# Bias tables ahead of x in SyncE's queue, three late W_up chunks, one product ahead of the first row factors, and remainders moved in W_out's second half

## The chip, the core and the metric

The kernel runs on one core of one Trainium2 chip. The metric is the time of one execution in device microseconds; lower is better. TensorE (PE) multiplies, VectorE (DVE) and ScalarE (ACT) do elementwise work, GpSimd (POOL) does small vectors and some transfers, and SyncE (SP) issues most DMAs.

## The reference

One encoder layer on a sequence of 512 positions and 1024 channels, in float32:

```python
h = rms_norm(x, attn_norm_g)
xr, gate, q, k, v = split(h @ w_in)             # 512 columns each
xr = centred_depthwise_conv(xr, conv_w, conv_b)
y_rnn = (rg_lru(xr, fwd) + rg_lru(xr, bwd)) * gelu(gate)
y_attn = dilated_attention(q, k, v, rel_bias)   # 8 heads, three dilated windows
mix = concat(rms_norm(y_rnn), rms_norm(y_attn))
x = x + mix @ w_out
x = x + square(relu(rms_norm(x) @ w_up)) @ w_down
return rms_norm(x)
```

## The kernel before, in words

**Products in three parts.** Every float32 operand is split into a rounded part and a remainder, `hi` and `lo`; `mm3` (L322 to L325) makes one product of three matmuls: hi·hi, hi·lo, lo·hi. A weight chunk of 128 x 1024 goes through three steps: a load into `wraw`, `tw` or a piece of `ws`; `conv_hi` (L252, on ACT, a few on DVE) writes `whi`; `conv_lo` (L279, on DVE) writes `wlo` as the difference. `whi` and `wlo` have four buffers each and `wraw` has three, so a step waits until the step or product that used the buffer before has gone by. `remake` (L262, L264) is another way to a remainder: ACT writes the negative rounded part, and a POOL transfer adds the raw chunk to it.

**Who sets the order.** On PE, ACT, DVE and POOL the order of the program is the order of the engine. SP's queue is ordered by the framework and runs ahead of the other engines; its issues wait only for buffers and for the landing of DMAs issued earlier. `emit_dma` (L230) issues the next chunk of the list `plain` into a `wraw`; it is called by `conv_lo`, so that each chunk that is done fetches another. The list runs over w_in, w_v, w_out and then w_up.

**Start.** x arrives transposed, in eight pieces, with the first columns of w_in. `cvx` splits them, and PE multiplies (`pxr`, four banks of PSUM). The sums of squares are turned by PE (`pcs`, L441), added by DVE (`cs`, `rv`), raised to the power -0.5 by POOL (`rcol`, L428, 128 x 4), turned back by four transposes (`prow`, L420) and copied by ACT (`rrow`): the first row factors. `xmm` makes the products of the fourth bank, k = 1 to 7, around that place. Convolution (`conv_a`, `conv_b`, L516 to L525) and the gates' products (`pg`, L544) follow.

**Attention.** For a pair of heads and a block of queries, `att_s` (L830) makes the scores in two banks, one for each head, and `att_e` (L847) adds the bias and takes the minimum on DVE and the exponential on ACT. The bias comes as a table for each head and parity in a `tw` buffer; `load_tw` fetches it with two DMAs from `nbd` in DRAM (L496, 192 KB, and L498, 160 KB). There are four `tw` buffers. Between these steps `fill` draws from a list of products (`pqk`, and `pwo` of W_out's first half) and `add_x` draws from the list `more`. `load_x` fills `more` with the loads of x in rows (`x_in`, L1078, 256 KB each), of blocks of W_out (`w_in`, L1081, 512 KB each), and sums of these (`sum1` to `sum3`).

**W_out's second half** takes seven steps, `OSEQ = 11, s2, s3, s4, 21, s1, 22`, of four products each. `wo_x` (L1231) adds a finished bank to x. The steps 11, s2, s3 and s4 use the same pair of banks, so a product of s2 waits until `wo_x` has read what 11 left there; and `wo_x` needs the factors of the attention half, `rc[1]`, which come over the same way as the first: `pcs`, `cs`, `rv`, POOL's `rcol`. `BES` names what is done beside each product: `conv_hi`, `conv_lo`, the remainders `o_lo`, `o_lo2` (L931, L937) of the attention output, and `st["wo"]`, which adds the last bank of W_out's first half to x (L1014). Then come w_up and w_down, which the diff does not touch.

Of the kernel before, what the change touches and what calls it, by code (L numbers as in the profile page):

```python
# [12 lines left out]
FT = mybir.dt.float32  # L13
# [4 lines left out]
P = 128  # L18
# [85 lines left out]
def hybrid_kernel(ctx: ExitStack, tc, xw0, xw, xn, w_in, w_v, w_out, w_up, w_dn, gates, vecs, rel, onehot, fg, out):  # L104
# [13 lines left out]
    def g_(name, dt=FT, shape=(P, S)):  # L118
        return work.tile(list(shape), dt, name=name, tag="g", bufs=NG)
# [111 lines left out]
    def emit_dma():  # L231
        if plain:
            i = plain.popleft()
            r = stream.tile([P, 1024], FT, name="wraw", tag="wraw", bufs=3)
            nc.sync.dma_start(r, source(chunks[i]))
            raws[i] = r
# [8 lines left out]
    def conv_hi(i):  # L245
        if i < len(chunks):
            i = swap.get(i, i)
            hi = stream.tile([P, 1024], FR, name="whi", tag="whi", bufs=4)
            if i in ON_DVE:
                nc.vector.tensor_copy(hi, raws[i])  # L250
            else:
                act(hi, raws[i], AF.Copy)  # L252
            splits[i] = (hi,)
# [9 lines left out]
        for n, t in enumerate(remade[i]):  # L263
            nc.gpsimd.dma_start(f(t), raws[i][:, n * S:(n + 1) * S], accum_op=OP.add)  # L264

    def emit_plain(i):
        if chunks[i] == ("o", "11"):
            emit_dma()

    def conv_lo(i):  # L270
        if i < len(chunks):
            i = swap.get(i, i)
            r = raws.pop(i)
            if i in remade:
                splits[i] += (remade.pop(i),)
                emit_plain(i)
                return
            lo = stream.tile([P, 1024], FR, name="wlo", tag="wlo", bufs=4)
            nc.vector.tensor_tensor(lo, r, f(splits[i][0]), op=OP.subtract)  # L279
            splits[i] += (lo,)  # L280
            c = chunks[i]
            if isinstance(c, tuple) and c[0] == "o":
                if c[1] == "11":
                    emit_dma()
            elif isinstance(c, tuple) and len(c) == 4:
                h, kind, f0 = c[:3]
                if kind == "t1" and cq[h, f0, "t2"] not in raws:
                    nc.gpsimd.dma_start(r, ublock(h, "22", f0), accum_op=OP.add)
                    raws[cq[h, f0, "t2"]] = r
                elif kind == "22":  # L290
                    t = raws[cq[h, f0, "t3"]]
                    nc.vector.tensor_tensor(t, t, r, op=OP.add)
                elif kind in ("t2", "21"):
                    held[kind] = r
                    if len(held) == 2:
                        t = held.pop("t2")
                        nc.vector.tensor_tensor(t, t, held.pop("21"), op=OP.add)
                        raws[cq[h, f0, "t4"]] = t
                        emit_dma()
                if kind in ("11", "22"):  # L300
                    emit_dma()
            elif isinstance(c, tuple) and c[1][0] == "s":
                nxt = {"s1": ("s2", "22"), "s2": ("s4", "21")}.get(c[1])
                if nxt:
                    nc.gpsimd.dma_start(r, wblock(c[0], nxt[1], c[2]), accum_op=OP.add)
                    raws[cd_[c[0]] + {"s2": 2 * NQ + 2 * c[2], "s4": 6 * NQ + c[2]}[nxt[0]]] = r
            else:
                emit_dma()

    def feed(c, k):  # L310
# [24 lines left out]
    h_lo = big.tile([P, KD, S], FR, name="h_lo", tag="bigB")  # L335

    XW, XG = S + 3 * P, S + KD
    xwt, w3 = [], []
    for k in range(KD):
        if 4 <= k < 7:  # L340
            xwt.append(stream.tile([P, 1024], FT, name="wraw", tag="wraw", bufs=3)[:, :XW])
        else:
            xwt.append(work.tile([P, 1024], FT, name="tw", tag="tw", bufs=4)[:, :XW if k else XG + 3 * P])
        if k == 0:
            nc.sync.dma_start(xwt[0][:, :XG], xw0[:, :XG])
            nc.sync.dma_start(xwt[0][:, XG:], xw0[:, XG:])
            w03 = g_("w03")[:, :P]
            nc.sync.dma_start(w03, w_in[3][:, :P])
        else:
            nc.sync.dma_start(xwt[k], xw[k - 1])  # L350
        if k == 6:
            nc.sync.dma_start(vt, vecs)
    ag = consts.tile([P, KD], FT, name="ag")
    nc.gpsimd.tensor_copy(ag, xwt[0][:, S:XG])

    sqx = {}

# [318 lines left out]
    def xmm(ks):  # L676
        for k in ks:
            mm3(pxr[3], wk(3, k), hk(k), False, k == KD - 1)
# [7 lines left out]
    for i in range(2):  # L686
        nc.gpsimd.dma_start(oht[i], onehot[:, i * S:(i + 1) * S])
    conv_lo(4)
    xmm(range(1, 2))
    rstd = row_tile(rcol, "et")  # L690
    conv_a(0, pxr[0])
    conv_a(1, pxr[1])
# [1 line left out]
    cneg, chalf = next(spc)  # L694
    conv_b(0)
    act(warm, epsb, AF.Sigmoid)
    xmm(range(2, KD))
    conv_a(2, pxr[2])
    conv_a(3, pxr[3])
    conv_lo(5)  # L700
# [232 lines left out]
    def o_hi2(k):  # L933
        act(o_tiles(k)[0], at[2 + k], AF.Copy)
# [74 lines left out]
    def wo_thunks():  # L1009
        order = [(0, tt, k) for tt in range(4) for k in range(4)] + [(1, tt, k) for h in (0, 2) for tt in range(4) for k in (h, h + 1)]  # L1010
        pw = {}

        def end(n, tt):
            stt(x1[tt, n], pw[n, tt], rc[0][:, tt:tt + 1], x1[tt, n], op0=OP.mult, op1=OP.add)  # L1014

        def mk(b, n, tt, k):
            def run():
                if k == 0:
                    pw[n, tt] = ps_("pwo", "pj")
                o = pw[n, tt]  # L1020
                hi, lo = splits[C_WO + 2 * n + k // 2]
                sl, tsl = slice((k % 2) * S, (k % 2 + 1) * S), slice(tt * P, (tt + 1) * P)
                mm3(o, [t[:, tsl] for t in ycat[k]], (hi[:, sl], lo[:, sl]), k == 0, k == 3)
                if b in (1, 15, 18, 28):
                    conv_hi(C_WO + {1: 3, 15: 4, 18: 5, 28: 6}[b])
                if b in (3, 17, 20):
                    conv_lo(C_WO + {3: 3, 17: 4, 20: 5}[b])
                if n == 0 and tt and k == 3:
                    end(0, tt - 1)
                if n and (tt, k) == (0, 1):  # L1030
                    end(0, 3)
                if n and k == 3 and tt < 3:
                    end(1, tt)
            return run
        st["wo"] = lambda: end(1, 3)
        return [mk(b, *o) for b, o in enumerate(order)]
# [11 lines left out]
    def fill(n):  # L1048
        for _ in range(n):
            if fillers and fillers[0] is None:  # L1050
                fillers.popleft()
                load_x()
            if fillers:
                fillers.popleft()()
# [12 lines left out]
    def load_x():  # L1067
        xb = big.tile([P, KD, S], FT, name="x1", tag="bigA")
        ws = big.tile([P, 4, 1024], FT, name="ws", tag="bigB")
        b12, b22, b21, s1 = [ws[:, i, :] for i in range(4)]  # L1070
        tt = nc.vector.tensor_tensor

        def chunk(n, t):
            raws[C_WA + OSEQ.index(n)] = t

        def x_in(g, n):
            x1[g, n] = xb[:, 2 * g + n, :]
            return lambda: nc.sync.dma_start(x1[g, n], xn[2 * g + n])  # L1078

        def w_in(t, b):  # L1080
            return lambda: nc.sync.dma_start(t, oblock(b))  # L1081

        def sum1():
            tt(s1, b12, raws[C_WA], op=OP.add)

        def sum2():
            t = work.tile([P, 1024], FT, name="tw", tag="tw", bufs=4)
            tt(t, s1, b22, op=OP.add)
            chunk("s2", t)
            t4 = work.tile([P, 1024], FT, name="tw", tag="tw", bufs=4)  # L1090
            chunk("s4", t4)
            more[1].append(lambda: tt(t4, t, b21, op=OP.add))

        def sum3():
            tt(b12, b12, b22, op=OP.add)

        for n, t in (("s3", b12), ("22", b22), ("21", b21), ("s1", s1)):
            chunk(n, t)
        w_in(b12, "12")()
        x_in(0, 0)()  # L1100
        more.append([x_in(1, 0), w_in(b22, "22")])
        more.append([x_in(2, 0), x_in(3, 0)])
        more.append([sum1, w_in(b21, "21")])
        more.append([sum2, x_in(0, 1)])
        more.append([sum3, x_in(1, 1)])
        more.append([x_in(2, 1), x_in(3, 1)])

    def rnn_end(t):
        last[t]()
# [137 lines left out]
        nc.vector.tensor_tensor(hb["l"][k], hm[k], f(hb["h"])[:, k, :], op=OP.subtract)  # L1247

    fill(1)
    att_av(3, range(4))  # L1250
    fill(1)
    o_sum("s1", 1)
# [5 lines left out]
    fill(3)  # L1258
    rc[1] = rstd_cols(row_sums(turned(ssy[1], "gs")), S)
    fill(1)  # L1260
    conv_lo(C_WA + 2)
    remake(C_WA + OSEQ.index("21"))
    fill(len(fillers))
    nrc = consts.tile([P, 4], FT, name="nrc")
# [3 lines left out]
        return {0: lambda: conv_hi(C_WA + j), 3: lambda: conv_lo(C_WA + j)}  # L1268

    BES = {w: cv(i + 3) for i, w in enumerate(OSEQ)}  # L1270
    BES["11"].update({1: lambda: (o_hi2(1), remake(C_WA + OSEQ.index("s1"))), 3: lambda: st["wo"]()})
    BES["s2"].update({1: lambda: conv_lo(C_WA + 3), 2: lambda: o_hi("s1", 1), 3: lambda: (conv_lo(C_WA + 4), o_lo2(0))})
    BES["s3"].update({1: lambda: o_lo2(1)})
    BES["s4"].update({1: lambda: (o_lo("s1", 0), o_sum("22", 1)), 2: lambda: o_hi("22", 1)})
    BES["21"].update({1: lambda: o_lo("s1", 1), 3: lambda: (conv_lo(C_WA + 7), o_lo("22", 0), o_lo("22", 1))})
    BES["s1"].update({1: lambda: h2_t(0, "pj"), 2: lambda: h2_t(1, "pj"), 3: lambda: (conv_lo(C_WA + 8), h2_l(0))})
# [558 lines left out]
```

## Time and profile before

| | us |
|---|---|
| median of 3 runs | 535.21 |
| lowest and highest | 534.62, 536.07 |
| profiled execution, its own time | 536.4 |
| span of its profile, first to last instruction | 534.6 |
| PE busy | 525.5 |
| DVE busy | 434.6 |
| ACT busy | 359.1 |
| POOL busy | 72.3 |

The profile is of one execution. The mean granted clock of TensorE is 0.999 of full speed. A line of the timeline gives the start, the duration, the engine, the line of the kernel, the operation, what it writes and reads, and in brackets how long the engine was idle before and what ended that. SPq marks the issue of a DMA, not its transfer. The end of a matmul is modelled, so what a wait cost PE is read from the starts of two matmuls that follow each other.

### The profile page before, as it was taken

What the parts mean: (1) busy time and instruction counts of PE and PEld (TensorE: products, weight loads), DVE (VectorE), ACT (ScalarE), POOL (GpSimd) and SP (SyncE); (2) the same over time, 40 slices, a digit from 0 to 9 for tenths busy, and PEclk for the clock granted to TensorE, in tenths of its full rate; (3) what the DMA queues carried; (4) which work ended last, traced back from release to release, by engine and by line L of the source; (5) the groups of instructions that cost most, each with busy time, mean ns of one, the idle gap of its engine ahead of it and who ended that gap; (6) DMA issues with size and microseconds to landing.
All of it is one profiled execution on the core that took longest, in us unless ns stands there. A gap on an engine that the chain in (4) does not pass through costs nothing.

```text
span 534.6 us, 8387 instructions
## 1 busy us (share of the span) xinstructions
PE 525.5 (98%) x3035; PEld 451.3 (84%) x3035; DVE 434.6 (81%) x640; ACT 359.1 (67%) x578; POOL 72.3 (14%) x121
## 2 busy tenths in 40 slices
PE   9999999999998999999999999999999999999995
PEld 7756888887886778889999888888999999888884
DVE  5999788986866789889769986879756987987885
ACT  6578946787865666587567755566657686755664
POOL 0282000000100051001030213001101110131000
PEclk9999999999999999999999999999999999999999
DMA  8754386598687259956595899995978496799704
GB/s 280 220 151 139 81 228 186 158 242 216 148 287 245 67 90 207 366 199 167 153 191 165 201 262 275 292 347 114 289 229 209 115 217 193 176 297 258 192 1 158
DMA packets 42602, 107.05 MB, mean 200 GB/s; under 512 B 4916, under 2 KB 15284, under 8 KB 42560
## 3 DMA queue, kind: packets, MB, share of 16 engines
q1 hardware_dynamic: 34848, 80.14, 46.0%
q0 software_dynamic: 7536, 26.14, 26.3%
q8 instruction: 24, 0.39, 0.3%
q10 hardware_dynamic: 176, 0.23, 0.1%
q14 instruction: 18, 0.15, 0.1%
HBM read 94.92 MB, written 4.23 MB: 185 GB/s over the span
## 4 chain that ended last, share of the span: by engine, by line
PE 85%; issue 8%; DVE 3%; DMA 1%; POOL 1%; SPq 0%; ACT 0%; DVEq 0%; POOLq 0%; ACTq 0%
PE pu L324 10%; PE pu L323 10%; PE pu L325 10%; PE pd L323 9%; PE pd L324 9%; PE pd L325 9%; PE pqk L323 3%; PE pqk L325 3%; PE pqk L324 3%; PE ps L830 2%; PE pv L323 2%; PE pg L544 1%; PE pv L324 1%; PE pp L323 1%; PE pp L325 1%
## 5 line engine op out<-in xcount | busy, mean ns | idle before, releaser
L279 DVE TENSOR_TENSOR wlo<-wraw,whi 128x1024 fp32r<-128x1024 f32 x71 | 86.7, 1221 | 23.2 <-ACT whi L252 22.8
L252 ACT ACTIVATE whi<-wraw 128x1024 fp32r<-128x1024 f32 x67 | 70.8, 1059 | 37.0 <-PE pd L325 19.3
L324 PE MATMUL pd<-wlo,ah 128*128 128x512 f32 (+1 forms) x195 | 75.3, 386 | 0.0
L323 PE MATMUL pd<-whi,ah 128*128 128x512 f32 (+1 forms) x195 | 75.3, 386 | 0.0
L325 PE MATMUL pd<-whi,al 128*128 128x512 f32 (+1 forms) x195 | 75.3, 386 | 0.0
L252 ACT ACTIVATE whi<-tw 128x1024 fp32r<-128x1024 f32 x38 | 40.2, 1060 | 39.4 <-DMA tw<-in_w_up_dram 12.0
L324 PE MATMUL pu<-hl,whi 128*128 128x256 f32 x224 | 63.5, 283 | 0.0
L325 PE MATMUL pu<-hh,wlo 128*128 128x256 f32 x224 | 63.4, 283 | 0.0
L323 PE MATMUL pu<-hh,whi 128*128 128x256 f32 x224 | 63.4, 283 | 0.0
L279 DVE TENSOR_TENSOR wlo<-tw,whi 128x1024 fp32r<-128x1024 f32 x38 | 46.5, 1222 | 19.1 <-ACT whi L252 19.1
L323 PE MATMUL pu<-h2h,whi 128*128 128x256 f32 (+1 forms) x200 | 60.1, 301 | 0.0
L324 PE MATMUL pu<-h2l,whi 128*128 128x256 f32 (+1 forms) x200 | 60.1, 300 | 0.0
L325 PE MATMUL pu<-h2h,wlo 128*128 128x256 f32 (+1 forms) x200 | 60.0, 300 | 0.0
L324 PEld LDWEIGHTS pu<-hl,whi 128*128 128x128 f32 x224 | 43.0, 192 | 0.0
L323 PEld LDWEIGHTS pu<-hh,whi 128*128 128x128 f32 x224 | 43.0, 192 | 0.0
L325 PEld LDWEIGHTS pu<-hh,wlo 128*128 128x128 f32 x224 | 43.0, 192 | 0.0
L325 PEld LDWEIGHTS pd<-whi,al 128*128 128x128 f32 x195 | 36.6, 188 | 7.4
L323 PEld LDWEIGHTS pd<-whi,ah 128*128 128x128 f32 x195 | 36.6, 188 | 7.3
L324 PEld LDWEIGHTS pd<-wlo,ah 128*128 128x128 f32 x195 | 36.6, 188 | 7.3
L252 ACT ACTIVATE whi<-ts 128x1024 fp32r<-128x1024 f32 x24 | 25.5, 1061 | 24.2 <-PE pd L325 18.4
L323 PEld LDWEIGHTS pu<-h2h,whi 128*128 128x128 f32 x200 | 38.3, 191 | 1.3
L325 PEld LDWEIGHTS pu<-h2h,wlo 128*128 128x128 f32 x200 | 38.3, 191 | 1.3
(282 smaller groups left out, 1259.7 us busy)
## 6 DMA issues: line engine op xcount, KB each, us to landing
wraw<-in_w_up_dram SPq DMA_DIRECT2D x25, 512.0 KB, 4.4
ts<-in_w_dn_dram POOLq DMA_DIRECT2D x24, 512.0 KB, 13.6
wraw<-in_w_dn_dram SPq DMA_DIRECT2D x24, 512.0 KB, 6.6
tw<-in_w_up_dram SPq DMA_DIRECT2D x15, 512.0 KB, 6.9
tw<-in_w_up_dram POOLq DMA_DIRECT2D x15, 512.0 KB, 8.4
wraw<-in_w_in_dram SPq DMA_DIRECT2D x13, 512.0 KB, 3.8
ts<-in_w_dn_dram SPq DMA_DIRECT2D x8, 512.0 KB, 7.8
tw<-in_w_dn_dram SPq DMA_DIRECT2D x8, 512.0 KB, 6.5
```

The costliest lines, as they stand in the source:

```text
L252: act(hi, raws[i], AF.Copy)
L279: nc.vector.tensor_tensor(lo, r, f(splits[i][0]), op=OP.subtract)
L323: nc.tensor.matmul(o, lhsT=a[0], rhs=b[0], start=bool(first), stop=False, skip_group_check=on)
L324: nc.tensor.matmul(o, lhsT=a[0], rhs=b[1], start=False, stop=False, skip_group_check=on)
L325: nc.tensor.matmul(o, lhsT=a[1], rhs=b[0], start=False, stop=bool(last), skip_group_check=on)
L544: nc.tensor.matmul(pg[2 * d + j][halves[b ^ d]], lhsT=gwr[t][halves[b], c], rhs=xc[t][halves[b]], start=True, stop=True)
L830: nc.tensor.matmul(psq[p][e][:, :NK], lhsT=sp[p, 0, n, e][:, c0:c0 + P], rhs=k, start=i == 0, stop=i == 1)
```

## The change

- In `load_x`, the second entry of `more` becomes empty and the loads of x's third and fourth piece move to the third entry. In SP's queue they come behind the four DMAs of the last pair's bias tables, where they were ahead of them.
- Three calls of `emit_dma` go from `conv_lo` (for W_out's chunks 2 and 3 and for the block 11) to three new entries at the end of `more`. The three w_up chunks that they issue come behind all loads of x in SP's queue; two of them were ahead of the bias tables. `emit_plain` goes.
- `xmm` makes the products k = 1 and 2 ahead of the transposes of the first row factors, where it made k = 1.
- The split of the block s3 moves: `conv_hi` from beside product 28 of W_out's first half to beside product 23, and `conv_lo` from behind the row factors of the attention half to ahead of the last attention product. Where it was, `o_lo2(0)` stands now; `o_lo2(1)` moves from s3 to s2; `conv_lo` of s4 moves from s2 to 11; `st["wo"]` moves from 11 to the end of s3.
- The copy of `ag` on POOL stands earlier in the program; on POOL it is in the same place.

No operation is added or removed on any engine. On SP one more pair moves by itself: the last two copies of `xcs` (L535) now come ahead of a w_in chunk, not behind it.

```diff
-    def emit_plain(i):
-        if chunks[i] == ("o", "11"):
-            emit_dma()
-
     def conv_lo(i):
...
             if i in remade:
                 splits[i] += (remade.pop(i),)
-                emit_plain(i)
                 return
...
             if isinstance(c, tuple) and c[0] == "o":
-                if c[1] == "11":
-                    emit_dma()
-            elif isinstance(c, tuple) and len(c) == 4:
+                return
+            if isinstance(c, tuple) and len(c) == 4:
...
-            else:
+            elif i not in (C_WO + 2, C_WO + 3):
                 emit_dma()
...
+            nc.gpsimd.tensor_copy(ag, xwt[0][:, S:XG])
             w03 = g_("w03")[:, :P]
...
-    xmm(range(1, 2))
+    xmm(range(1, 3))
     rstd = row_tile(rcol, "et")
...
-    xmm(range(2, KD))
+    xmm(range(3, KD))
...
-                if b in (1, 15, 18, 28):
-                    conv_hi(C_WO + {1: 3, 15: 4, 18: 5, 28: 6}[b])
+                if b in (1, 15, 18, 23):
+                    conv_hi(C_WO + {1: 3, 15: 4, 18: 5, 23: 6}[b])
...
-        more.append([x_in(2, 0), x_in(3, 0)])
-        more.append([sum1, w_in(b21, "21")])
+        more.append([])
+        more.append([sum1, x_in(2, 0), x_in(3, 0), w_in(b21, "21")])
         more.append([sum2, x_in(0, 1)])
         more.append([sum3, x_in(1, 1)])
         more.append([x_in(2, 1), x_in(3, 1)])
+        more.append([emit_dma])
+        more.append([emit_dma])
+        more.append([emit_dma])
...
     fill(1)
+    conv_lo(C_WA + 2)
     att_av(3, range(4))
...
-    conv_lo(C_WA + 2)
+    o_lo2(0)
     remake(C_WA + OSEQ.index("21"))
...
-    BES["11"].update({1: lambda: (o_hi2(1), remake(C_WA + OSEQ.index("s1"))), 3: lambda: st["wo"]()})
-    BES["s2"].update({1: lambda: conv_lo(C_WA + 3), 2: lambda: o_hi("s1", 1), 3: lambda: (conv_lo(C_WA + 4), o_lo2(0))})
-    BES["s3"].update({1: lambda: o_lo2(1)})
+    BES["11"].update({1: lambda: (o_hi2(1), remake(C_WA + OSEQ.index("s1")))})
+    BES["s2"].update({2: lambda: o_hi("s1", 1), 3: lambda: (conv_lo(C_WA + 4), o_lo2(1))})
+    BES["s3"][3] = lambda: (conv_lo(C_WA + 5), st["wo"]())
```

More of the change, by code (lines that the diff above doesn't have):

```diff
@@ L337, in hybrid_kernel @@
     XW, XG = S + 3 * P, S + KD
+    ag = consts.tile([P, KD], FT, name="ag")
     xwt, w3 = [], []
@@ L352, in hybrid_kernel @@
             nc.sync.dma_start(vt, vecs)
-    ag = consts.tile([P, KD], FT, name="ag")
-    nc.gpsimd.tensor_copy(ag, xwt[0][:, S:XG])
     sqx = {}
```

## The prediction

> **What bounds the kernel now.** I read the page first, then the waits of PE, then the timeline around each of those waits.
>
> ```profile
> span 534.6 us, 8387 instructions
> ...
> PE 525.5 (98%) x3035; PEld 451.3 (84%) x3035; DVE 434.6 (81%) x640; ACT 359.1 (67%) x578; POOL 72.3 (14%) x121
> ```
> ```profile
> PE ps L830 <- DVE mn L847: 1.3, 1, 1.3
> ...
> PE prow L420 <- POOL rcol L428: 0.4, 1, 0.4
> ...
> PE pwo L323 <- DVE x L1231: 0.2, 1, 0.2
> ```
>
> PE is busy for 98% of the span, and the matmuls stay. So the end moves only by what PE loses in waits, and the list of its waits (its last column is the longest one) names three behind the start. The change touches the surroundings of all three. I price each by the starts of neighbouring matmuls.
>
> **First row factors.**
>
> ```profile
> 23.01 1.34 POOL L428 TENSOR_TENSOR rcol<-rv,mhalf 128x4 f32<-128x4 f32 x1 [19.17 <-DVE rv L425]
> ...
> 23.37 0.39 PE L324 MATMUL pxr<-h_lo,whi 128*128 128x512 f32 x1
> ...
> 23.60 0.39 PE L325 MATMUL pxr<-h_hi,wlo 128*128 128x512 f32 x1
> ...
> 24.40 0.65 PE L420 MATMUL prow<-ident,rcol 128*128 128x128 f32 x4 [0.41 <-POOL rcol L428]
> ...
> 33.43 0.75 DVE L525 SCALAR_TENSOR_TENSOR xc<-xr,vt,xc 128x511 f32<-128x511 f32 x1
> ...
> 35.28 1.95 PE L544 MATMUL pg<-xc,gwr 64*64 64x512 f32 x16
> ```
>
> Matmuls of this size follow each other by 23.60 - 23.37 = 0.23. Here 24.40 - 23.60 = 0.80 pass: 0.57 lost, because the transposes wait for POOL, which ends at 23.01 + 1.34 = 24.35. The change puts the product k = 2 there: three matmuls, 0.69, of operands that the product before it uses too or that are older. It runs from 23.83 to 24.52, so the transposes find POOL done: gain 0.57. The transposes themselves come 0.12 later, and what hangs on them does too, while the products behind come 0.57 earlier. The nearest product that needs that chain is the second group of gates at 35.28, which needs the convolution ending at 33.43 + 0.75 = 34.18. That margin of 1.10 shrinks by 0.69 to 0.41 and hides it. Without that cover the gain would sink by up to 0.57, to nothing. I take 0.57.
>
> Two small pieces of this stretch cost nothing. The copy of `ag` keeps its place on POOL. And two copies of `xcs` pass a w_in chunk in SP's queue:
>
> ```profile
> 39.81 0.33 SPq L235 DMA_DIRECT2D wraw<-in_w_in_dram  x1
> ...
> 51.23 0.69 DVE L250 CAST whi<-wraw 128x1024 fp32r<-128x1024 f32 x1
> ```
>
> DVE takes up that chunk at 51.23, 11 after its issue, and two issues ahead of it take about 1.2 (as the key copies below).
>
> **Bias tables, x and w_up chunks in SP's queue.**
>
> ```profile
> 143.09 0.54 SPq L235 DMA_DIRECT2D wraw<-in_w_up_dram  x1
> ...
> 149.46 1.22 SPq L805 DMA_DIRECT2D kk<-kk  x2
> 150.76 0.68 SPq L235 DMA_DIRECT2D wraw<-in_w_up_dram  x1
> 151.85 1.78 SPq L1078 DMA_DIRECT2D x<-in_xn_dram  x2
> 153.96 0.33 SPq L496 DMA_DIRECT2D tw<-nbd  x1
> ...
> 156.30 0.43 SPq L498 DMA_DIRECT2D tw<-nbd  x1
> ```
> ```profile
> 147.08 0.08 DVE L847 DVE_READ_ACCUMULATOR2_ANT mn<- 128x1 f32 x1
> ...
> 154.03 0.75 DVE L1014 SCALAR_TENSOR_TENSOR x<-pwo,rcol,x 128x512 f32<-128x512 f32 x1 [0.99 <-DMA x<-in_xn_dram]
> ...
> 157.38 0.35 PE L830 MATMUL ps<-kk,qh 128*128 128x416 f32 x1
> ...
> 157.56 0.35 PE L830 MATMUL ps<-kk,ql 128*128 128x416 f32 x1
> ...
> 161.36 0.35 PE L830 MATMUL ps<-kk,ql 128*128 128x416 f32 x1
> ...
> 162.41 0.59 DVE L847 CUSTOM_DVE_ANT_0 e<-ps,tw 128x416 f32<-128x416 f32 x1 [1.40 <-DMA tw<-nbd]
> ...
> 163.06 0.45 PE L830 MATMUL ps<-kk,qh 128*128 128x416 f32 x1 [1.35 <-DVE mn L847]
> ...
> 165.08 0.75 DVE L1014 SCALAR_TENSOR_TENSOR x<-pwo,rcol,x 128x512 f32<-128x512 f32 x1
> ```
>
> Score matmuls follow by 157.56 - 157.38 = 0.18; here 163.06 - 161.36 = 1.70 pass: 1.52 lost. PE wants a bank that DVE still reads, and DVE sat idle for the bias table. That table's last DMA was issued at 156.30 and landed when DVE went on, at 162.41: about 6.1 of transfer. Ahead of it in the queue stand a w_up chunk of 512 KB at 150.76, needed by nobody for 50 us, and two pieces of x.
>
> In the new order both come behind the tables, and so does the chunk at 143.09. The buffers are free from 147.08 + 0.08, so the first table DMA can follow the key copies (149.46 + 1.22 = 150.68) at about 150.7 instead of 153.96. If the last keeps its distance of 2.34 from the first, it goes out at 153.0, 3.3 earlier, and with the old 6.1 it lands at 159.1. PE, ahead by 0.57, asks for the bank at 161.36 + 0.18 - 0.57 = 160.97; DVE takes 0.59; so the table is in time until about 160.4. That is 1.3 to spare: gain 1.52. The other end: SP's issues also wait for the landing of earlier DMAs, and if the last table has to wait for x's first piece, which came at 154.03 in the old order, it lands at 160.1, still in time, by 0.3. Only if the tables come no earlier at all is the 1.52 lost.
>
> Moved behind them, x's third piece is wanted at 165.08, now some 2.1 earlier, at 163.0; issued by 155 and taking the same 6.1 it lands at 161.1. The DVE work in between hides it.
>
> **Row factors of the attention half, and the moved remainders.**
>
> ```profile
> 136.94 1.04 POOL L428 TENSOR_TENSOR rcol<-rv,mhalf 128x4 f32<-128x4 f32 x1 [11.72 <-DVE rv L425]
> ...
> 181.84 0.62 ACT L934 ACTIVATE oh<-at 128x512 fp32r<-128x512 f32 x1
> ...
> 184.30 0.69 DVE L976 TENSOR_TENSOR yp<-pav,zrow 128x512 f32<-128x512 f32 x1 [1.24 <-PE pav L970]
> ...
> 185.03 0.72 ACT L990 ACTIVATE at<-yp,vt 128x512 f32<-128x512 f32 x1 [1.96 <-DVE yp L976]
> ...
> 187.06 1.04 ACT L252 ACTIVATE whi<-ws 128x1024 fp32r<-128x1024 f32 x1
> ...
> 189.67 1.22 DVE L279 TENSOR_TENSOR wlo<-ws,whi 128x1024 fp32r<-128x1024 f32 x1
> ...
> 189.84 1.91 POOL L428 TENSOR_TENSOR rcol<-rv,mhalf 128x4 f32<-128x4 f32 x1 [25.90 <-DVE rv L425]
> ...
> 191.86 0.74 DVE L1231 SCALAR_TENSOR_TENSOR x<-pwo,rcol,x 128x512 f32<-128x512 f32 x1
> ...
> 192.03 0.39 PE L325 MATMUL pwo<-whi,ol 128*128 128x512 f32 x1
> ...
> 192.66 0.50 PE L323 MATMUL pwo<-whi,oh 128*128 128x512 f32 x1 [0.25 <-DVE x L1231]
> ...
> 196.82 0.68 DVE L937 TENSOR_TENSOR ol<-at,oh 128x512 fp32r<-128x512 f32 x1
> ```
>
> Here 192.66 - 192.03 = 0.63 pass instead of 0.23: 0.40 lost. PE waits for DVE's 191.86 + 0.74 = 192.60, which waits for POOL's power, 189.84 to 191.75. The same power on the same four columns took 1.04 at 136.94. At 189.84 it took 1.91, and DVE was subtracting a whole chunk from 189.67 to 190.89; the power ends 0.86 after that. I read it as POOL being held up by DVE. The change puts the half-sized subtraction of 0.68 (196.82) in that place. It ends at 190.35, 0.54 earlier, so the power ends by 191.21 and DVE's addition by 192.06, ahead of the 192.26 at which PE comes without a wait. Gain 0.40. If the power takes 1.91 whatever DVE does, the gain is 0.
>
> The Trainium skill, page "SBUF — State Buffer", section "Who interferes with whom", says that a VectorE instruction with two SBUF inputs contends with a GpSimd instruction that reads SBUF, and that the later one is blocked to the end of the first. The rows 136.94 and 189.84 agree with it. By that rule the 0.40 would go; by the longest duration in the rows it would stay, and the sum would be smaller by it.
>
> The chunk's subtraction must go elsewhere: into DVE's idle 1.24 ahead of 184.30. It takes 1.22, so it fits with 0.02 to spare, provided that its `whi` is there. ACT makes that in 1.04 from about 181.84, done at 182.9, before DVE is free at 183.06; ACT's idle 1.96 ahead of 185.03 hides it. If it did not fit, everything from 184.30 to the power would be late by up to 1.22. I take 0. The last addition of W_out's first half (0.74 on DVE) moves behind s3; its bank is next wanted in the step 21, over 2 us later.
>
> **Sum.** 0.57 + 1.52 + 0.40 = 2.49. The profiled execution took 536.4, its span 534.6 with 1.8 around it; it lies 1.2 above the median of the runs, 535.21. From the median: 535.2 - 2.5 = 532.7. A difference under 0.3%, 1.6 us, I count as none.
>
> **Rivals.**
> - Tables no earlier (the change doesn't do what it says): SP's issues stay tied to landings. 1.52 stays: 534.2. Against it: the 1.3 to spare. Chance 0.10.
> - The power takes its 1.91 anyway: 0.40 stays, 533.1. For it: its first instance, at 23.01, took 1.34, so its length varies. Chance 0.08.
> - The moved subtraction doesn't fit: `yp` and the row factors behind it come up to 1.22 late, the shorter subtraction beside POOL gives 0.54 of that back, and the last wait grows by 0.68 instead of going: 0.57 + 1.52 - 0.68 = 1.41, 533.8. For it: 0.02 to spare. Chance 0.06.
> - PE arrives 2.5 early at engines and transfers that keep their own pace, and waits there: 535.2. Against it: no further wait of PE is listed, and later loads start when a product frees a buffer. Chance 0.08.
> - Slower: a held w_up chunk comes too late for the up-projection. Three chunks are to be split before that starts, the first here:
>
> ```profile
> 168.61 0.33 SPq L235 DMA_DIRECT2D wraw<-in_w_up_dram  x1
> ...
> 201.81 1.05 ACT L252 ACTIVATE whi<-wraw 128x1024 fp32r<-128x1024 f32 x1
> ```
>
> The third of these chunks already goes out at 168.61. If the first, held back to the same place, isn't landed by 201.81 - 2.5 = 199.3, each further microsecond stops PE; past 2.5 it is slower than before, past 4.1 by more than 0.3%, say 537.0 at 4.3. That needs 30 us from issue to landing, where the table above took 6. Chance 0.05.
>
> **How the numbers follow.** The forecast has 0.63. Its own range is 532.1 to 533.6, since the runs of before lie up to 0.6 below and 0.9 above their median. The range of all cases goes from 531.9, for waits too small to be listed that may go too, to 534.5, 0.3 beyond the highest of the first three rivals: it takes in the tables, the power and the subtraction, and leaves out the gain waited away and the slower case. Faster: 0.63 + 0.08, so 0.71. Same: 0.10 + 0.06 + 0.08 = 0.24. Slower: 0.05.
>
> **What would show it.** In the profile after: transposes at 24.5 with no idle time ahead, then all of PE 0.57 early; the tables' four issues right behind the key copies, and no DVE wait for `tw` near 162; no gap between score matmuls near 160.5; the last power nearer to 1.4 than to 1.9, the step s2 following 11 at 0.23, and the first w_up chunk split about 2.5 before 201.81. Wrong: a DVE wait for `tw` or x over 1 us in that stage, `yp` over 0.2 behind its product, a PE wait for W_up's chunks, or a PE wait over 0.3 that is not in the list above.

## The result and the profile after

The changed kernel takes 532.88 us, median of 8 runs (532.20 to 534.43), against 535.16 for the kernel before in the same rounds (534.62 to 536.61): 2.28 us less, a ratio of 0.9956 with a 95% interval of 0.9941 to 0.9970 (the ratios here are not simply those of the two medians). The forecast was 532.7. In a second set of rounds the two stood at 532.70 and 534.40, 1.70 us apart, ratio 0.9973 (0.9961 to 0.9984). Its first profiled execution took 533.1 with a span of 531.4, 3.2 us less than the span before: more than either median, and why is the main question of the experiments.

The head of the page after, and the whole list of PE's waits:

```profile
span 531.4 us, 8385 instructions
...
PE 524.4 (99%) x3035; PEld 452.3 (85%) x3035; DVE 434.3 (82%) x640; ACT 358.4 (67%) x578; POOL 71.7 (13%) x121
```
```profile
PE pwarm L147 <- PEq L1822: 0.8, 1, 0.8
```

The three waits that the prediction named are gone, and no other of a length that the list names has come in their place; what is left is the warm-up at the start. Line numbers up to L252 are the same; behind it they are lower by up to 6: L422 is the old L428, L841 the old L847, L1228 the old L1231.

The timeline after, at the first row factors:

```profile
22.55 1.33 POOL L422 TENSOR_TENSOR rcol<-rv,mhalf 128x4 f32<-128x4 f32 x1 [18.87 <-DVE rv L419]
...
23.82 0.39 PE L319 MATMUL pxr<-h_hi,wlo 128*128 128x512 f32 x1
24.05 0.60 PE L414 MATMUL prow<-ident,rcol 128*128 128x128 f32 x4
...
33.03 0.75 DVE L519 SCALAR_TENSOR_TENSOR xc<-xr,vt,xc 128x511 f32<-128x511 f32 x1
...
34.19 0.66 PE L538 MATMUL pg<-xc,gwr 64*64 64x512 f32 x4
```

POOL ends at 22.55 + 1.33 = 23.88, the added product runs until the transposes follow at 24.05, 0.23 behind its last matmul and with no idle time. The margin of the second gates group is 34.19 - (33.03 + 0.75) = 0.41, as forecast.

At the bias tables (SP's issues, the last score matmuls, DVE's work on them):

```profile
146.84 1.25 SPq L799 DMA_DIRECT2D kk<-kk  x2
148.14 0.58 SPq L490 DMA_DIRECT2D tw<-nbd  x1
...
150.64 0.37 SPq L492 DMA_DIRECT2D tw<-nbd  x1
151.33 1.64 SPq L1072 DMA_DIRECT2D x<-in_xn_dram  x2
...
160.06 0.90 SPq L235 DMA_DIRECT2D wraw<-in_w_up_dram  x2
```
```profile
160.38 0.35 PE L824 MATMUL ps<-kk,qh 128*128 128x416 f32 x1
...
160.57 0.35 PE L824 MATMUL ps<-kk,ql 128*128 128x416 f32 x1
...
160.58 0.59 DVE L841 CUSTOM_DVE_ANT_0 e<-ps,tw 128x416 f32<-128x416 f32 x1 [1.46 <-PE ps L824]
```

The four table DMAs follow the key copies, the last at 150.64 where it was 156.30. What had held them is in the landings: in the trace before, each of the four went out 0.02 behind the landing of the eighth DMA ahead of it in SP's queue (153.94, x's first piece; 154.61; 155.91; 156.28, a key copy). In the trace after, that landing is past when the first two go out (148.14 and 148.78); the last two still pause for 0.50 and 0.32, and the landings eight places ahead of them are not in the trace. The score matmuls have their pitch of 0.19, and DVE now waits for PE (`ps`), not for a table.

At the last row factors and the first held W_up chunk:

```profile
180.17 1.22 DVE L274 TENSOR_TENSOR wlo<-ws,whi 128x1024 fp32r<-128x1024 f32 x1
...
181.35 0.50 PE L317 MATMUL pwo<-whi,yh 128*128 128x512 f32 x1
...
181.50 0.69 DVE L970 TENSOR_TENSOR yp<-pav,zrow 128x512 f32<-128x512 f32 x1
...
186.86 0.68 DVE L931 TENSOR_TENSOR ol<-at,oh 128x512 fp32r<-128x512 f32 x1
...
187.03 1.38 POOL L422 TENSOR_TENSOR rcol<-rv,mhalf 128x4 f32<-128x4 f32 x1 [26.06 <-DVE rv L419]
```
```profile
189.22 0.39 PE L319 MATMUL pwo<-whi,ol 128*128 128x512 f32 x1
...
189.45 0.40 PE L317 MATMUL pwo<-whi,oh 128*128 128x512 f32 x1
```
```profile
198.56 1.05 ACT L252 ACTIVATE whi<-wraw 128x1024 fp32r<-128x1024 f32 x1
```

The power takes 1.38, the step s2 follows 11 at 0.23. The moved subtraction ends at 181.39 and `yp` starts at 181.50, 0.15 behind the matmul that follows the sums of the attention, as in the trace before (184.30 behind 184.16). The first W_up chunk is split at 198.56, 3.25 earlier than before, with no wait.

### The profile page after: what moved, and what is told of

It is laid out like the page before. It is cut to its first block, busy times and chain, and to the rows that moved or that the text cites. A ratio compares the mean times of both kernels' runs of the same rounds, so it can differ in the third digit from the quotient of the medians.

```text
span 531.4 us, 8385 instructions
## 1 busy us (share of the span) xinstructions
PE 524.4 (99%) x3035; PEld 452.3 (85%) x3035; DVE 434.3 (82%) x640; ACT 358.4 (67%) x578; POOL 71.7 (13%) x121
## 4 chain that ended last, share of the span: by engine, by line
PE 86%; DVE 5%; ACT 4%; DMA 2%; issue 2%; SPq 0%; DVEq 0%; ACTq 0%
PE pu L318 10%; PE pu L317 10%; PE pu L319 10%; PE pd L317 10%; PE pd L318 9%; PE pd L319 9%; PE pwo L317 3%; PE pt L862 3%; PE pwo L319 3%; PE pwo L318 3%; PE pav L964 2%; PE ps L824 2%; DVE wlo L274 1%; PE pg L538 1%; PE pqk L317 1%
## 5 line engine op out<-in xcount | busy, mean ns | idle before, releaser
L252 ACT ACTIVATE whi<-wraw 128x1024 fp32r<-128x1024 f32 x67 | 70.8, 1058 | 34.9 <-PE pd L319 18.2
L252 ACT ACTIVATE whi<-tw 128x1024 fp32r<-128x1024 f32 x38 | 40.1, 1059 | 40.6 <-DMA tw<-in_w_up_dram 13.2
L252 ACT ACTIVATE whi<-ts 128x1024 fp32r<-128x1024 f32 x24 | 25.5, 1061 | 26.0 <-PE pd L319 18.6
```

## The experiments

PE's work is the same in all kernels, so I divide each trace at five pairs of matmuls and compare the distances of their starts: A to the first turn of the column sums (`pcs`), B from there to the first `pv` (first row factors), C from the first scores `ps` to the first `pav`, D from the last pair's fourth score step to the step 11 (the late table), E from there to the first `pxt` (the step s2). A begins at the start of the span. All other distances repeat within 0.15 us in the 14 traces, the longest of them, 323 us, included.

| kernel | A | B | C | D | E |
|---|---|---|---|---|---|
| before | 21.32 | 7.69 | 33.91 | 28.46 | 15.75 |
| e8_before, the same kernel | 20.82 | 7.66 | 33.86 | 27.17 | 15.75 |
| after | 20.86 | 7.06 | 33.95 | 26.73 | 15.22 |
| e10_after, the same kernel | 20.11 | 7.08 | 33.83 | 26.73 | 15.19 |
| e1_product | 20.97 | 7.08 | 33.79 | 27.64 | 15.72 |
| e2_queue | 21.15 | 7.70 | 33.28 | 26.72 | 15.71 |
| e3_wout | 20.42 | 7.69 | 33.33 | 27.41 | 15.18 |
| e4_behind | 21.54 | 7.71 | 33.81 | 27.81 | 15.59 |
| e5_held | 21.21 | 7.69 | 34.22 | 26.73 | 15.73 |
| e6_xmove | 21.00 | 7.68 | 34.39 | 27.19 | 15.73 |
| e7_reduce | 21.39 | 7.69 | 33.81 | 27.92 | 15.59 |
| e9_noqueue | 21.17 | 7.08 | 33.35 | 27.06 | 15.18 |
| e11_hold2 | 20.53 | 7.06 | 33.28 | 26.73 | 15.19 |
| e12_hold2b | 20.93 | 7.69 | 33.28 | 27.40 | 15.75 |

B and E fall into two groups with nothing between but the 15.59 explained below. A, C and D differ from run to run, D only where the old queue or a part of it is left. That also tells where the 3.2 us between the two first profiles came from: A gave 0.46, which no edit touches, and D gave 1.73, since the first trace has the longest D of all.

**e1_product.** The first row factors alone.

```diff
-    xmm(range(1, 2))
+    xmm(range(1, 3))
...
-    xmm(range(2, KD))
+    xmm(range(3, KD))
```

> The kernel before with one edit alone: the products k = 1 and 2 ahead of the first transposes. Theory (the three losses are local and come out at the end one for one): the 0.57 us ahead of the transposes goes, the transposes start about 0.12 later than before, the second gates product and everything behind it 0.57 earlier, the median 0.6 us below before. Rival A (of the 1.10 that the second gates product moved in the changed kernel, all is this edit): 1.1 us. Rival B (the gates wait instead, or POOL's power gets longer and the transposes still wait): 0 to 0.3 us. The other two waits, 1.52 and 0.40, stand as before in all cases.

Median 534.10 against 534.69, ratio 0.9988 (0.9979 to 0.9996): 0.59 us. PE's waits:

```profile
PE ps L830 <- DVE mn L847: 0.6, 1, 0.6
PE pwo L323 <- DVE x L1231: 0.2, 1, 0.2
```

The wait of the transposes is gone, the other two stand; B is 0.61 shorter. The step is worth its forecast. But the wait for the table is 0.6 where the kernel before showed 1.3, and nothing near it was changed.

**e2_queue.** The edits of SP's queue alone (of the diff above, `conv_lo`, `emit_plain` and `more`).

> The kernel before with the edits of SyncE's queue alone: x's third and fourth piece behind the tables, three W_up chunks behind all x. Theory: the last table DMA lands about 5 us earlier than the 162.2 of before, the gap of 1.70 us between score matmuls near 161 goes to 0.18, the median falls by 1.5 us. Rival A (PE comes 1.5 us early and waits for something behind it, such as the loads of x or the held W_up chunks): under 0.8 us, with a new wait of PE. Rival B (the changed kernel's own gain there, 1.72 us, holds small gains beside the wait): 1.7 us.

Median 534.02 against 534.69, ratio 0.9985 (0.9976 to 0.9994): 0.67 us, less than half of what was expected. PE's waits:

```profile
PE prow L414 <- POOL rcol L422: 0.4, 1, 0.4
PE pwo L317 <- DVE x L1228: 0.2, 1, 0.2
```

The table's wait is gone, no new one has come, and D is 26.72: rival A falls, though the time is the one that it gave; theory and rival B, with 1.5 and 1.7, missed it. The edit does in full what it says; what it took away was not 1.52 in most runs.

**e3_wout.** The moves around W_out's second half alone.

> The kernel before with the moves around W_out's second half alone. Theory: the half-size subtraction beside POOL's last power shortens it from 1.91 us to about 1.4, the step s2 follows 11 at 0.23 us, and the median falls by 0.4 us. Rival A (in the changed kernel the wait went because of the other parts): the wait of 0.40 stays, 0 us. Rival B (the chunk's subtraction doesn't fit ahead of the last sum of the attention, which in the changed kernel it did with no idle time left): yp late by up to 1.2 us, the median 0.3 to 0.7 us above before.

Median 534.18 against 534.69, ratio 0.9990 (0.9979 to 1.0000): 0.51 us. E is 0.57 shorter than before. The wait ahead of s2 is gone, with its 0.40. In the trace before, the matmul behind the one that had waited was late too, 0.34 behind 192.66 where the pitch is 0.23:

```profile
193.00 0.39 PE L324 MATMUL pwo<-wlo,oh 128*128 128x512 f32 x1
```

That is another 0.11. A smaller wait ahead of s3's third product (196.96, 0.31 behind its predecessor) is gone as well, but a similar one stands ahead of s3's first product now (0.28). The power:

```profile
187.10 0.69 DVE L937 TENSOR_TENSOR ol<-at,oh 128x512 fp32r<-128x512 f32 x1
...
187.27 1.38 POOL L428 TENSOR_TENSOR rcol<-rv,mhalf 128x4 f32<-128x4 f32 x1 [25.88 <-DVE rv L425]
```

Both rivals fall: the wait is gone without the other parts, and `yp` starts 0.14 behind the matmul that follows the attention's sums, as in the trace before.

**e4_behind.** No work on DVE beside the power.

```diff
-    conv_lo(C_WA + 2)
     remake(C_WA + OSEQ.index("21"))
...
-    BES["11"].update({1: lambda: (o_hi2(1), ...
+    BES["11"].update({1: lambda: (conv_lo(C_WA + 2), o_hi2(1), ...
```

> The kernel before with one move alone: the 128 x 1024 subtraction that DVE does while POOL raises the last row factors to their power goes behind the first addition that needs them, so that DVE idles beside the power. Theory (two-input DVE work holds POOL up): the power takes 1.0 to 1.1 us as at 136.94, ends at 190.9, the wait of 0.40 ahead of the step s2 goes, the median falls by 0.4 us, as much as all the moves of the changed kernel there bring. Rival (the power's length has other causes): it takes 1.9 us again, and the median stays within 0.1 us.

```profile
189.34 1.01 POOL L428 TENSOR_TENSOR rcol<-rv,mhalf 128x4 f32<-128x4 f32 x1 [25.88 <-DVE rv L425]
...
191.26 1.22 DVE L279 TENSOR_TENSOR wlo<-ws,whi 128x1024 fp32r<-128x1024 f32 x1
```
```profile
195.85 0.40 PE L325 MATMUL pwo<-whi,ol 128*128 128x512 f32 x1
...
196.30 0.50 PE L323 MATMUL pwo<-whi,oh 128*128 128x512 f32 x1
```

The power takes 1.01, as the theory has it, and the wait ahead of s2 is gone. But the median is 535.19 against 534.69, ratio 1.0000 (0.9989 to 1.0011), not 0.4 us lower: the subtraction at 191.26 now holds up the additions behind it. The third product of s2 comes 0.31 behind its predecessor (193.19) and the third of s3 0.45 (196.30), 0.08 and 0.22 beyond the pitch. E gains 0.16 in all, which the times can't show. So a short power alone is not enough: the subtraction must not stand ahead of these additions either, and the changed kernel's longer way, moving it ahead of the attention's sums, gives 0.54 (after) and 0.57 (e3_wout).

**e7_reduce.** As e4_behind, with a reduction of the same length beside the power.

```diff
+    nc.vector.tensor_reduce(small("red", 4), raws[C_WA + OSEQ.index("22")].rearrange(...), axis=X, op=OP.add)
     remake(C_WA + OSEQ.index("21"))
```

> As e4_behind, but DVE does something else beside POOL's last power: a reduction of 128 x 1024 numbers to 128 x 4, one input, whose result nothing uses; it adds one instruction of about 1.2 us to the kernel. In e4_behind the power took 1.01 beside an idle DVE, in the kernels with the 1.22 us subtraction beside it 1.91, with the 0.68 us subtraction 1.38. Theory (a second SBUF input holds POOL up; this reduction has one): 1.0 to 1.1 us. Rival (any work of DVE in SBUF holds POOL up; the first power took 1.34 beside a one-input cast): about 1.9 us, ending 0.86 after the reduction. The Trainium skill, page SBUF — State Buffer, section Who interferes with whom, would have 1.0: it names a second SBUF input, or a copy or cast in a two-port mode, and excepts the reduction.

```profile
189.10 1.22 DVE L1261 TENSOR_REDUCE red<-ws 128x4 f32<-128x1024 f32 x1
```
```profile
189.28 1.01 POOL L428 TENSOR_TENSOR rcol<-rv,mhalf 128x4 f32<-128x4 f32 x1 [25.90 <-DVE rv L425]
```

DVE is busy for 1.22 over as many numbers, and the power takes 1.01: not any work of DVE holds POOL up. One execution took 535.7. In the trace of before there is another case, at the first row factors:

```profile
22.76 0.69 DVE L250 CAST whi<-wraw 128x1024 fp32r<-128x1024 f32 x1
```

This cast has one input, and the power beside it took 1.34: it ended at 24.35, 0.90 behind the cast's end at 23.45. Behind the subtractions it ends 0.86 (before, 191.75 against 190.89) and 0.87 later (after, 188.41 against 187.54). So the cast looks to count like a two-input operation, and the first power's 1.34 to be the same effect: all 14 traces have it at 1.33 or 1.34, ending 0.90 behind that cast. No run takes the cast away, so this one is argued, not tested. The Trainium skill, page "SBUF — State Buffer", section "Who interferes with whom", names all three: two SBUF inputs, a copy or cast in a two-port mode, and the reduction as harmless; these rows agree. None of them shows in which mode the cast runs; it takes 0.69 for as many numbers as the subtraction does in 1.22.

**e5_held and e6_xmove.** The two halves of the queue's edit: the three W_up chunks held back, x where it was; and x's two pieces moved, the chunks where they were.

```diff
 # e6_xmove
-        more.append([x_in(2, 0), x_in(3, 0)])
-        more.append([sum1, w_in(b21, "21")])
+        more.append([])
+        more.append([sum1, x_in(2, 0), x_in(3, 0), w_in(b21, "21")])
```

> The kernel before with one half of the queue's edit: the three W_up chunks held back, x's third and fourth piece still ahead of the tables. So far four profiles with the old queue have the last table DMA landing 0.70 after, 0.00 after, 0.23 before and 0.18 after the moment at which PE wants the bank, and PE loses 1.52, 0.81, 0.58 and 0.98 us there; with both halves of the edit it lands about 3.0 us ahead and nothing is lost. Theory (what counts is the bytes that stand ahead in the queue; two chunks of 512 KB against two pieces of 256 KB): two thirds of the shift, so the table lands about 1.9 us ahead of that moment, nothing is lost, the median falls by as much as with the whole edit (0.7 us). Rival A (what counts is the number of DMAs ahead, two and two): half of the shift, 1.4 ahead, nothing is lost either. Rival B (x's pieces alone stand in the way): the loss stays at 0.6 to 1.5 us.

> The kernel before with the other half of the queue's edit: x's third and fourth piece behind the tables, the W_up chunks where they were. Theory (bytes): a third of the shift, the last table DMA lands about 0.9 us ahead of the moment at which PE wants the bank, give or take the 0.45 by which the landing differs between profiles; 0 to 0.4 us is lost of the 0.6 to 1.5. Rival A (number of DMAs): half of the shift, 1.4 ahead, nothing is lost. Rival B (the W_up chunks alone stand in the way): landing as before, 0.6 to 1.5 lost.

The last table's issue and the scores, first in e5_held, then in e6_xmove:

```profile
154.31 0.37 SPq L492 DMA_DIRECT2D tw<-nbd  x1
...
161.64 0.35 PE L824 MATMUL ps<-kk,qh 128*128 128x416 f32 x1
...
161.83 0.35 PE L824 MATMUL ps<-kk,ql 128*128 128x416 f32 x1
```
```profile
154.84 0.37 SPq L498 DMA_DIRECT2D tw<-nbd  x1
...
161.27 0.59 DVE L847 CUSTOM_DVE_ANT_0 e<-ps,tw 128x416 f32<-128x416 f32 x1 [1.39 <-DMA tw<-nbd]
161.40 0.35 PE L830 MATMUL ps<-kk,ql 128*128 128x416 f32 x1
...
161.92 0.46 PE L830 MATMUL ps<-kk,qh 128*128 128x416 f32 x1 [0.17 <-DVE mn L847]
```

With the chunks held, the last table lands at 159.6, 2.0 ahead of the moment at which PE wants the bank, and D is 26.73: nothing is lost. With only x moved it lands at 161.1, 0.5 ahead, and 0.34 is still lost. Two kernels with the whole old queue did as well: in e8_before (below) the last table lands 0.5 ahead and 0.35 is lost, in e9_noqueue 0.6 ahead and 0.23. So holding the chunks is enough to take the loss away, and that moving x helps at all is not shown: rival B of e6_xmove, the chunks alone in the way, is not excluded, since its 0.6 to 1.5 was narrower than what the old queue costs. Whether bytes or the count of DMAs ahead set the shift stays open. The medians can't tell: 534.36 and 534.89 against 534.58, ratios 0.9995 (0.9985 to 1.0004) and 1.0004 (0.9992 to 1.0016). In e5_held's profile a long C of 34.22 took back part of what D gave.

**e8_before.** The kernel before, once more.

> The kernel before, unchanged, for a fifth profile of the old queue and another of the start. Theory (the wait for the bias table differs from run to run, since the DMAs keep their own pace): a loss between 0.5 and 1.6 us between the score matmuls near 161, about 1.0 in the mean, and the transposes of the first row factors anywhere between 23.5 and 24.7. Rival (the 1.52 us is what this kernel loses; the other three profiles differ by their edits): 1.4 to 1.6 us.

```profile
160.52 0.59 DVE L847 CUSTOM_DVE_ANT_0 e<-ps,tw 128x416 f32<-128x416 f32 x1 [1.07 <-DMA tw<-nbd]
160.65 0.35 PE L830 MATMUL ps<-kk,ql 128*128 128x416 f32 x1
...
161.18 0.46 PE L830 MATMUL ps<-kk,qh 128*128 128x416 f32 x1 [0.18 <-DVE mn L847]
```

The same rows as in the prediction, and 161.18 - 160.65 = 0.53 instead of 1.70: 0.35 lost instead of 1.52. It lies below the range expected, and it ends the rival: the same kernel lost 1.52 in one execution and 0.35 in another. One run, 534.6.

**e9_noqueue and e10_after.** The changed kernel without the queue's edits, and the changed kernel itself.

> The changed kernel without the edits of SyncE's queue: the product ahead of the first row factors and the moves around W_out's second half alone. Six profiles with the old queue lost 1.52, 0.81, 0.58, 0.98, 1.07 and 0.34 us to the late bias table, 0.9 in the mean. Theory (the table's landing varies from run to run, and 1.52 was a late one): another loss in 0.3 to 1.5, the row factors' stretch 0.6 and the stretch around the step s2 0.5 shorter than before, the median 1.1 us below before and 0.9 to 1.0 above the changed kernel in the same rounds. Rival (1.52 to 1.7 is what the table usually costs): 1.5 to 1.7 above the changed kernel.

> The changed kernel, unchanged, in the same rounds. Theory (0.62 for the row factors, 0.9 to 1.0 for the table in the mean, 0.53 around s2): 2.1 us below before. Rival (the sum of the prediction holds, 2.5, or the 3.2 of the two first profiles): 2.5 or more below. Its profile: no loss between the score matmuls near 160, the stretch from the last scores to W_out's second half 26.7 us as in the three profiles with the table in time; the start up to the first column sums anywhere between 20.4 and 21.6.

e9_noqueue: 533.07 against 534.40, ratio 0.9975 (0.9966 to 0.9984), 1.33 us; 1.1 was expected. The changed kernel is 1.70 below before in these rounds, where 2.1 was expected and 2.5 or more by the rival; so it is 0.37 us faster than e9_noqueue, not 0.9 to 1.0. The profile of e9_noqueue had lost only this much:

```profile
159.91 0.35 PE L830 MATMUL ps<-kk,ql 128*128 128x416 f32 x1
...
160.32 0.46 PE L830 MATMUL ps<-kk,qh 128*128 128x416 f32 x1
```

0.41 - 0.18 = 0.23. Eight profiles with the old queue have D at 27.06 to 28.46, mean 27.61, 0.88 above the 26.73 of the five without a loss. The times of whole runs put it lower: 0.67 us in e2_queue, 0.22 in e5_held, which loses nothing there either, and 0.37 here. By its interval the first lies between 0.3 and 1.3, the second between -0.2 and 0.8; the third is a difference of two results that are each uncertain by half a microsecond. A mean of 0.9 lies within the first and a little beyond the second; 1.52 lies outside both.

**e11_hold2 and e12_hold2b.** The same remedy one pair of heads earlier, on the changed kernel and on the kernel before. In `conv_lo`, two chunks more don't emit the next; two calls of `emit_dma` stand in `plan` instead.

```diff
-            elif i not in (C_WO + 2, C_WO + 3):
+            elif i not in (C_QK + 6, C_QK + 7, C_WO + 2, C_WO + 3):
                 emit_dma()
...
+    for key in ((1, 0, 4), (1, 2, 4)):
+        plan.setdefault(key, []).append(emit_dma)
```

> The changed kernel and the same remedy one pair of heads earlier: a W_out chunk of 512 KB, which goes out near 105 ahead of the last piece of a bias table and is split near 124, is held back by one place, behind that piece. Eleven profiles so far spread over 1.1 us between the first scores and the first attention product (33.28 to 34.39), with PE waiting near 110 for a copy of ql and near 114 for z, which waits for that table. Theory: the second of these waits, 0 to 0.4 us, goes, the first stays, since ql stands ahead of the chunk: 0.1 to 0.3 us in the mean, 33.3 to 33.8 for that stretch. Rival (the transfers of the next tables are all late there, so one place changes nothing): 33.3 to 34.4 as before, no change of the median.

> The kernel before with the remedy of e11_hold2 alone: the W_out chunk near 105 one place later in SyncE's queue, behind the last piece of the table. In e11_hold2 the second copy of ql, issued ahead of both, took 5.07 us to land, where it took 5.7 to 6.0 in the other profiles, and the stretch from the first scores to the first attention product was 33.28, the shortest seen, as in four of thirteen. Theory (the chunk slows transfers issued shortly ahead of it too, so with the chunk later nothing is waited for in that stretch): ql in 5.0 to 5.2 us, 33.3 us for the stretch, the median 0.5 us below before, since the other profiles with the chunk ahead have 33.8 in the mean. Rival (33.28 was a lucky run): ql in 5.7 to 6.0 us, 33.3 to 34.4, no change of the median. The bias table near 161 is late as before in both cases, by 0.2 to 1.5.

SP's queue in e10_after and in e11_hold2:

```profile
103.27 0.46 SPq L803 DMA_DIRECT2D ql<-ql  x1
...
104.45 0.40 SPq L235 DMA_DIRECT2D wraw<-in_w_out_dram  x1
104.90 0.42 SPq L492 DMA_DIRECT2D tw<-nbd  x1
```
```profile
103.63 0.46 SPq L803 DMA_DIRECT2D ql<-ql  x1
...
104.77 0.42 SPq L492 DMA_DIRECT2D tw<-nbd  x1
105.29 0.41 SPq L235 DMA_DIRECT2D wraw<-in_w_out_dram  x1
```

The DMA view of the same stretch (size, us from issue to landing), for e10_after, e11_hold2 and e12_hold2b:

```profile
ql<-ql SPq DMA_DIRECT2D x1, 128.0 KB, 5.9
```
```profile
ql<-ql SPq DMA_DIRECT2D x1, 128.0 KB, 5.1
```
```profile
ql<-ql SPq DMA_DIRECT2D x1, 128.0 KB, 5.2
```

One exchange in the queue, 512 KB behind 160 KB, and the copy of `ql` that goes out ahead of both takes 0.7 to 0.8 less; in all twelve other traces it takes 5.7 to 6.0. The expectation of e11_hold2 had that copy unchanged, since it stands ahead of the chunk; that was wrong. C is 33.28 in both, where the twelve others have 33.28 to 34.39, mean 33.79. Three of those twelve have 33.28 to 33.35 too, so the short C could be luck in one trace; the copy's time sets these two apart from all others. e12_hold2b: 534.12 against 534.81, ratio 0.9989 (0.9978 to 1.0000), 0.69 us; 0.5 was expected, and its table is late by as much as ever (D 27.40). e11_hold2: 532.47 against 534.40, ratio 0.9964 (0.9952 to 0.9976), the fastest of all; it is 0.23 below the changed kernel in the same rounds, which these runs alone do not tell from none.

## Why the prediction was right or wrong

- **The bound.** Right: PE is busy for 99%, and each wait that went came out at the end. The parts add up: B, D and E give 0.62 + 0.88 + 0.54 = 2.04 us in the mean of the profiles, inside both measured intervals (1.6 to 3.2 and 0.9 to 2.1 us). The three parts taken alone were worth 0.59, 0.67 and 0.51 by the times, 1.77 together.
- **First row factors, 0.57.** Right. B is 0.62 shorter, the median of e1_product 0.59 lower. The margin at the second gates group shrank to 0.41, as worked out.
- **Bias tables, 1.52.** The mechanism was right, the term too large. It was read from one execution, in which the table was later than in any of the seven other profiles with this queue; the mean loss is 0.88 by D, and 0.2 to 0.7 by the times. The prediction treated a wait for a transfer as a fixed length, like the waits for engines beside it, which repeat. What held the tables back in the old order the prediction knew only in part: it named the loads ahead of them in the queue and, for the new order, one landing. In all eight traces with the old queue, each of the four table DMAs goes out within 0.05 of the landing of the eighth DMA ahead of it, the last one behind a key copy. So the table comes as late as those landings and its own transfer make it, and these differ from run to run. The forecast that the tables' first DMA follows the key copies at 150.7 was too careful: the key copies came 2.6 earlier, 1.1 of it because all of that trace is earlier there. The rest comes with the held chunks: the first key copy goes out 9.47 ahead of the score step (157.38 in the trace before) in all five traces with the chunks held, and 7.8 to 8.9 ahead in the others, e6_xmove among them. So the last table DMA went out at 150.64, not 153.0. x's first piece, whose landing the prediction had as the other bound, still stands ahead of the tables, as the eighth ahead of the last; it went out at 143.66 instead of 146.19, and the last table DMA was out long before the 154.03 that was feared.
- **The power, 0.40.** Right in mechanism, a little low in size. E is 0.54 shorter; 0.40 of it is the wait named, and 0.11 the matmul behind it, which follows at 0.34 where the prediction counted the pitch of 0.23; the small waits in s3 nearly cancel. The reading that DVE holds POOL up was tested: 1.91 beside the 1.22 subtraction, 1.38 beside the 0.68 one, 1.01 beside nothing and beside a reduction. The prediction took the 1.34 of the first instance as a sign for its rival, that the length varies whatever DVE does; that instance stood beside a cast, which is the likelier reason.
- **Edits at nothing.** The subtraction ahead of `yp` fitted, by as little as forecast. x's pieces and the held chunks made nobody wait.
- **Rivals.** Tables no earlier, power unchanged, subtraction too long, chunk too late: each is excluded by a row above. Of the gain waited away later nothing is seen.
- **The sum.** 2.49 was forecast, 2.28 and 1.70 measured. Its excess is the table's term, 1.52 where the profiles have 0.88; the other two were good to 0.15 us, both a little low. That the first set of rounds came so near to 2.49, and that both medians of the changed kernel lie within 0.2 of the forecast 532.7, is in part luck: the parts add up to 2.04, and the kernel before stood at 535.16 in one set and at 534.40 in the other.

What stays open: whether the times' 0.2 to 0.7 for the queue or the profiles' 0.88 is nearer the truth, whether moving x's pieces does anything, and what makes the transfers behind A, C and D differ from run to run.

## What to carry to other kernels

In these 14 traces the waits for an engine repeat to a few hundredths of a microsecond, the waits for a transfer do not: price the first from one profile, the second from several, or as a range from zero to what the one shows. Look in the queue for large loads that nobody needs soon and put them behind the small ones that somebody waits for; in e11_hold2 and e12_hold2b one place made the small one land 0.7 sooner. Count places as well as bytes: an issue can be held by the landing of a DMA that stands eight places ahead. Keep two-input DVE work, and by the one case here casts, away from a POOL operation on which the next step hangs, and check what the moved work holds up in its new place.

## What the runs showed of the hardware

- The start up to `pcs` took 20.11 to 21.54 us in 14 executions; stretches in which PE waits for no transfer repeat within 0.15.
- A transfer of 512 KB slows one that was issued ahead of it: `ql` took 5.1 and 5.2 us in the two traces with the chunk one place later, 5.7 to 6.0 in the twelve others.
- In SP's queue an issue waits for the landing of the eighth DMA ahead of it: in the trace after, x's piece goes out at 151.33, 0.02 behind the landing of the one issued at 145.45, with seven issues between. In no trace does an issue go out before the landing of the eighth ahead, where that landing is recorded (176 in each trace); some go out before that of the seventh.
- POOL's power on four columns ends 0.86 to 0.90 us behind a DVE cast or two-input subtraction that runs when it starts, and takes 1.01 to 1.05 where there is none, beside a reduction too.
- In W_out's second half the matmul behind one that PE waited for follows at 0.33 or 0.34 us, not at 0.23 (193.00 behind 192.66 before, and 196.63 behind 196.30 in e4_behind).
